# Copies for the weight sums, moves of key rows and the last stores issued by other engines than the loads

## The chip, the core and the metric

The kernel runs on one core of a Trainium2 chip. The metric is the device time of one execution in microseconds. A run's time is a little longer than the span in its profile, which goes from the first to the last instruction. A core has a matmul engine (TensorE, PE in the profile, with its weight loads as PEld), a vector engine (VectorE, DVE), an activation engine (ScalarE, ACT), a general engine (GpSimd, POOL) and SyncE (SP), which here only issues transfers. Each engine works through its own list of instructions in order. SyncE, ScalarE and GpSimd can each issue DMA transfers: the transfer itself is done by DMA engines, but the instruction that issues it stands in the issuing engine's list, and so does its wait.

## The reference, cut to what matters

Two layers over 528 tokens (16 learned ones and 512), each with two token mixers, a causal pooling and a latent attention with 8 heads:

```python
for l in range(DEPTH):                       # DEPTH = 2, D_MODEL = 1024
    h = rmsnorm(h_res, norm_gain[l])
    proj = h @ w_in[l]
    u_pool, z_pool, c_q, c_kv, k_rope, z_mla, g_pool, g_mla = jnp.split(proj, IN_SPLIT_POINTS, axis=-1)
    y_pool = (pool_mix(u_pool, pool_w_group[l], pool_scale[l]) * jax.nn.silu(z_pool)) @ pool_w_up[l]
    o_mla = mla(c_q, c_kv, k_rope, pos, g_qa, g_kva, w_q_b, w_kv_b, g_qn, g_kn)
    y_mla = (o_mla * jax.nn.silu(z_mla)) @ mla_w_up[l]
    merged = jax.nn.sigmoid(g_pool) * y_pool + jax.nn.sigmoid(g_mla) * y_mla
    h_res = h_res + merged @ w_out[l]
```

In `mla`, a head's key is 64 columns of its own and 32 rotated columns that all heads share; keys and queries are normalised per head.

## The kernel before, in words

Tokens lie along the free axis, features along the 128 partitions. Every product with a weight runs as three matmuls on halves of split numbers (`mm3`, L192, L195, L196): high by high, low by high, high by low.

**Weights.** A stream of products, `plan`, runs from the first projection to the last output. For each chunk of 128x512, `wload` has SyncE load 256 KB into one of three `raw` buffers (L115), ScalarE copies it to the high half `whi` (L187) and VectorE subtracts to get the low half `wlo` (L188). A load waits for a free `raw` buffer, which `wlo` gives back.

**The attention of a head.** `prep(h)` multiplies the head's key rows with a spread factor `bc` (L875), splits the product and moves the rotated query rows (L889). `head` computes scores, exponentials (L915, ScalarE) and has GpSimd scale the weights by their sums (`scale`, L922 and L923); `pv` transposes them on TensorE (L979) and multiplies with the values. Between these pieces the stream of products is run on (`gap`), so that TensorE always has work.

**Key rows.** `kn[p]` holds the own key columns of a pair of heads, 64 rows each; `kp` holds the rotated shared key in rows 64 to 128. For the even head of a pair, `lend` moves the first 64 rows of `kn[p]` into `kp` (L866) and the head reads `kp`. For the odd head, `prep` moves the shared rows from `kp` into the first 64 rows of `kn[p]` (L877) and the head reads `kn[p]`. There are 8 moves of each kind.

**Sums of weights.** Some products of the second layer's gates and of both output projections use sums and differences of weight blocks, so that fewer products are needed. `weight_sums` builds these sums in DRAM ahead of their use: 32 copies DRAM to DRAM (L356), and on top of each an adding transfer issued by GpSimd (L359). They are spread over the attention by `after(...)`.

**What sets the order.** Instructions are written in the order in which the Python code runs, with a clock of planned matmul time (`clk`). A list scheduler then sets the final order on each engine, and waits follow from the data. `behind(ins, other)` adds a wait for another instruction by hand, and `earlier(ns)` names the matmul that was written `ns` of planned time ago. So `behind(x, earlier(14000))` lets x go when TensorE has come to 14 us of planned time before the place where x was written.

**The end.** The last products, named "ob", store their results with `self.out(..., q)` (L1101) on a queue that `out_pairs` chooses; the earlier outputs go out on GpSimd.

Of the kernel before, what the change touches and what calls it, by code (L numbers as in the profile page):

```python
# [72 lines left out]
def trunk(ctx, tc, xT, pos, win, wkr, wqb, wkb, wvb, wgr, wpu, wmu, wout, gains, const, yT):  # L73
    nc = tc.nc
    pe, act, dve, gp, sp = nc.tensor, nc.scalar, nc.vector, nc.gpsimd, nc.sync
# [15 lines left out]
    def slot(tag, dt=F32, bufs=1, w=W):  # L91
        return sl.tile([P, w], dt, tag=tag, name=nm(tag), bufs=bufs)

    def tmp(w=W):
        return tp.tile([P, w], F32, tag="tmp", name=nm("tmp"), bufs=3)
# [95 lines left out]
    def mm3(out, wh, wl, xh, xl, start, stop, more=False, hold=False):  # L191
        first = pe.matmul(out, wh, xh, start=start, stop=False, skip_group_check=more)  # L192
        if hold:
            behind(first, newest[0])
        pe.matmul(out, wh, xl, start=False, stop=False, skip_group_check=more)  # L195
        newest[0] = pe.matmul(out, wl, xh, start=False, stop=stop, skip_group_check=more)  # L196
        past.append((clk[0], newest[0]))
# [3 lines left out]
    def earlier(ns):  # L201
        return next((m for c, m in reversed(past) if c <= clk[0] - ns), past[0][1])
# [99 lines left out]
    def split(hi, lo, src, a, b):  # L302
        act.activation(hi[:, a:b], src, AF.Copy)  # L303
        dve.tensor_sub(lo[:, a:b], src, hi[:, a:b].bitcast(F32))  # L304

    def behind(ins, other):
        tc.add_manual_dep(ins.ins, other.ins.name,
                          mybir.DependencyInfo(mybir.DependencyClass.Sync, mybir.DependencyReason.DATA))
# [38 lines left out]
    def weight_sums(name, w):  # L347
        def made(u, i):
            a, b = w[2 * u], w[2 * u + 1]
            d = wsum[name][u]  # L350
            src = {0: (b[:, 0:512], b[:, 512:1024]), 2: (a[:, 0:512], b[:, 0:512]), 1: (a[:, 0:512], d[:, 0, :]),
                   3: (a[:, 512:1024], d[:, 1, :])}
            return d[:, i, :], src[i]

        def copy(d, src):
            behind(sp.dma_start(d, src[0]), earlier(14000))  # L356

        def add(d, src):
            behind(gp.dma_start(d, src[1], accum_op=ALU.add), earlier(4000))  # L359

        for u in range(len(w) // 2):
            for fn, i in ((copy, 0), (copy, 2), (add, 0), (copy, 1), (add, 2), (add, 1), (copy, 3), (add, 3)):
                yield lambda fn=fn, u=u, i=i: fn(*made(u, i))

    class Layer:
# [497 lines left out]
            sp.dma_start(bc, kdr[self.l][h:h + 1, :].partition_broadcast(P))  # L863

        def lend(self, p):
            sp.dma_start(self.kp[0:64, :], self.kn[p][0:64, :])  # L866

        def prep(self, h):
            p, odd = h // 2, h % 2
            n0, r0 = (64, 0) if odd else (0, 64)  # L870
            kf = tmp()
            bc = self.bcs.pop(h)
            if h + 2 < H:
                self.spread_k(h + 2)
            dve.tensor_mul(kf, self.kn[p] if odd else self.kp, bc)  # L875
            if not odd:
                sp.dma_start(self.kn[p][0:64, :], self.kp[64:128, :])  # L877
            elif p < 3:
                self.lend(p + 1)
            kh, kl = slot("kh", F32R, bufs=2), slot("kl", F32R, bufs=2)  # L880
            split(kh, kl, kf[:, :T], 0, T)
            qh, ql = qhl[odd]
            x0 = self.x0
            src = self.qn[p][n0:n0 + 64, x0:T]
            act.activation(qh[n0:n0 + 64, x0:T], src, AF.Copy)
            dve.tensor_sub(ql[n0:n0 + 64, x0:T], src, qh[n0:n0 + 64, x0:T].bitcast(F32))
            g0 = 32 * (h % 4)
            for d, f in zip((qh, ql), self.qr[h // 4]):
                sp.dma_start(d[r0:r0 + 32, x0:T].bitcast(F32), f[g0:g0 + 32, x0:T].bitcast(F32))  # L889
            return kh, kl, qh, ql  # L890
# [252 lines left out]
        def out_pairs(self, nxt, name, products):  # L1143
            order = [(p, u) for p in products for u in range(2)]
            l = self.l
            a, b, c = self.halves()
            n = b - a
            A, B = (a, b), (b, c)
            src = []
            for p, u in order:  # L1150
                w0, w1 = wout[l, OUT[2 * u]], wout[l, OUT[2 * u + 1]]
                src.append({1: w0[:, 0:512], 2: w0[:, 512:1024], 4: w1[:, 512:1024]}.get(p))
                if src[-1] is None:
                    src[-1] = wsum[l][u][:, {5: 0, 6: 1, 7: 2, 3: 3}[p], :]
            bank = self.banks

            def grow(m, s, v):
                x = xb[:, m, s[0]:s[1]]
                dve.scalar_tensor_tensor(out=x, in0=v, scalar=0.5, in1=x, op0=ALU.mult, op1=ALU.add)

            def carry(m, s, v, u, scale, o):
                t = self.carried[u][:, o:o + n]
                act.activation(t, v, AF.Copy, scale=scale)
                gp.dma_start(xb[:, m, s[0]:s[1]], t, accum_op=ALU.add)

            def body(i, w):
                p, u = order[i]
                m0, m1 = OUT[2 * u:2 * u + 2]
                key = {2: "e", 7: "c", 4: "c"}.get(p, "a"), u
                if key not in bank:  # L1170
                    bank[key] = (sct if key[0] == "a" else mmt)()
                ps = bank[key][:, :n]
                t, o = (B if p == 3 else A), (0 if p == 1 else 4)
                for k in range(4):
                    xh, xl = (x[:, t[0]:t[1]] for x in self.mg[k + o]) if p < 4 else self.tt[k][p]
                    c_ = P * k
                    mm3(ps, w[0][:, c_:c_ + P], w[1][:, c_:c_ + P], xh, xl, k == 0 and p in (1, 2, 7), k == 3, True)
                    if k == 1:
                        yield 6 * (n / 2.4)
                q = sp if name == "ob" else gp  # L1180
                if p == 1:
                    self.carried[u] = slot("sv", bufs=2)
                    carry(m0, A, ps, u, 0.5, 0)
                elif p == 2:
                    grow(m0, A, ps)
                    self.out(m0, A, nxt, q)
                elif p == 7:
                    grow(m1, B, ps)
                elif p == 6:
                    carry(m1, A, ps, u, -0.5, HALF)  # L1190
                elif p == 5:
                    carry(m1, B, ps, u, -0.5, 0)
                    self.out(m1, B, nxt, q)
                    if u == 1 and not self.last:
                        for m in range(3):
                            nxt.square_x(m)
                elif p == 4:
                    grow(m1, A, ps)
                    self.out(m1, A, nxt, q)
                else:  # L1200
                    grow(m0, B, ps)
                    self.out(m0, B, nxt, q)
                    if not self.last:
                        nxt.square_x(m0)
                        nxt.square_x(m1)
                if i == len(order) - 1:
                    done.add((l, name))
                yield 6 * (n / 2.4)

            plan.append(Gemm((l, name), src, 512 * len(src), body=body))  # L1210
            plan[-1].more = True

# [236 lines left out]
```

## Time and profile before

| | us |
|---|---|
| median of 3 runs | 782.33 |
| lowest and highest of them | 780.72, 783.87 |
| the profiled execution | 782.78 |
| its span | 781.0 |

| engine | busy us | share of the span |
|---|---|---|
| TensorE | 774.8 | 99% |
| VectorE | 568.6 | 73% |
| ScalarE | 445.2 | 57% |
| GpSimd | 233.3 | 30% |

Busy time counts the records of instructions, issuing a DMA not included on SyncE and ScalarE. Matmul records overlap, so TensorE can lose a few tenths of a microsecond between two starts and still read as busy. A wait is named by who waited and for whom; SyncE has no work of its own, so its waits are those of its queue of transfers. The transfers that the change concerns, from the page's list of DMA issues (output <- input, issuing queue, count, size, median us from issue to landing):

```profile
wsum<-wout SPq DMA_DIRECT2D x16, 256.0 KB, 3.5
wsumgp<-win SPq DMA_DIRECT2D x16, 256.0 KB, 3.3
kp<-kn SPq DMA_DIRECT2D x8, 132.0 KB, 5.2
yT<-xb SPq DMA_DIRECT2D x4, 128.0 KB, 1.7
```

### The profile page before, as it was taken

How to read it: one execution, taken by the hardware profiler on the slowest of the kernel's cores; microseconds unless marked ns; L12 is line 12 of the kernel's file. 1: busy time of each engine (PE TensorE's matmuls, PEld its weight loads, DVE VectorE, ACT ScalarE, POOL GpSimd, SP SyncE). 2: the span in 40 equal slices, each digit the busy share in tenths (PEclk: the TensorE clock that was granted, in tenths of full speed). 3: DMA queues.
4: the chain of work that ended last, by engine and by line, in shares of the span. 5: the costliest groups of instructions: out<-in, count | busy, mean ns of one | idle time of the engine just before them, and what ended most of it. 6: DMA issues, size and time to landing. Idle time of an engine off the chain costs nothing.

```text
span 781.0 us, 15326 instructions
## 1 busy us (share of the span) xinstructions
PE 774.8 (99%) x5469; PEld 712.5 (91%) x5469; DVE 568.6 (73%) x1326; ACT 445.2 (57%) x1016; POOL 233.3 (30%) x303
## 2 busy tenths in 40 slices
PE   9999999999999999999999999999999999999998
PEld 9999899999999999999997898887788999988887
DVE  5848787446778876589764477865897888864984
ACT  7645555645566665645564356546667766664462
POOL 1024525103335333211330136221006625440213
PEclk9999999999999999999999999999999999999999
DMA  6242467765746465565662524425556666662655
GB/s 244 82 97 89 124 170 151 179 167 144 156 109 165 115 141 120 155 168 175 168 170 81 98 87 123 132 63 181 141 140 162 174 174 166 176 221 75 209 154 138
DMA packets 65325, 112.92 MB, mean 145 GB/s; under 512 B 10704, under 2 KB 15696, under 8 KB 65248
## 3 DMA queue, kind: packets, MB, share of 16 engines
q1 hardware_dynamic: 55344, 92.18, 40.0%
q0 software_dynamic: 8896, 17.92, 13.0%
q10 hardware_dynamic: 1008, 1.84, 0.6%
q8 instruction: 43, 0.70, 0.4%
q14 instruction: 34, 0.28, 0.1%
HBM read 100.18 MB, written 22.62 MB: 157 GB/s over the span
## 4 chain that ended last, share of the span: by engine, by line
PE 92%; DVE 3%; DMA 2%; ACT 1%; issue 1%; SPq 0%; DVEq 0%; ACTq 0%
PE mm L192 26%; PE mm L196 26%; PE mm L195 26%; PE S L192 3%; PE S L196 2%; PE S L195 2%; PE mm L979 2%; PE o L985 1%; PE o L984 1%; DVE wlo L188 1%; PE S L506 1%; DMA raw<-win 1%; PE mm L408 1%; DMA raw<-wsum 1%; PE mm L465 0%
## 5 line engine op out<-in xcount | busy, mean ns | idle before, releaser
L192 PE MATMUL mm<-hh,whi 128*128 128x264 f32 (+2 forms) x992 | 307.0, 312 | 0.1
L196 PE MATMUL mm<-hh,wlo 128*128 128x264 f32 (+2 forms) x992 | 304.7, 309 | 0.3 <-DVE wlo L188 0.2
L195 PE MATMUL mm<-hl,whi 128*128 128x264 f32 (+2 forms) x992 | 304.4, 308 | 0.0
L188 DVE TENSOR_TENSOR wlo<-raw,whi 128x512 fp32r<-128x512 f32 (+1 forms) x253 | 179.8, 714 | 103.7 <-ACT whi L187 101.2
L187 ACT ACTIVATE whi<-raw 128x512 fp32r<-128x512 f32 (+1 forms) x253 | 154.2, 612 | 166.4 <-PE mm L195 105.0
L192 PEld LDWEIGHTS mm<-hh,whi 128*128 128x128 f32 x992 | 186.6, 189 | 11.0 <-ACT racc L993 0.5
L195 PEld LDWEIGHTS mm<-hl,whi 128*128 128x128 f32 x992 | 187.2, 189 | 8.7
L196 PEld LDWEIGHTS mm<-hh,wlo 128*128 128x128 f32 x992 | 186.2, 188 | 9.4 <-DVE wlo L188 1.1
L922 POOL TENSOR_SCALAR pa<-pa,rs 128x272 f32<-128x272 f32 (+1 forms) x32 | 33.0, 1031 | 103.0 <-DVE rs L941 64.2
L922 POOL TENSOR_SCALAR cq<-cq,rs 128x400 f32<-128x400 f32 (+1 forms) x32 | 52.2, 1631 | 0.0
L192 PE MATMUL mm<-cq,whi 128*128 128x264 f32 (+2 forms) x140 | 43.8, 313 | 0.0
L195 PE MATMUL mm<-cq,whi 128*128 128x264 f32 (+2 forms) x140 | 43.7, 312 | 0.0
L196 PE MATMUL mm<-cq,wlo 128*128 128x264 f32 (+2 forms) x140 | 43.3, 312 | 0.1
L908 DVE CUSTOM_DVE_ANT_0 S<-S,maskw,nqs 128x272 f32<-128x272 f32 (+4 forms) x80 | 38.6, 497 | 5.2 <-PE S L196 4.9
L725 POOL TENSOR_TENSOR racc<-racc,tmp 128x264 f32<-128x264 f32 (+1 forms) x15 | 14.5, 964 | 84.9 <-ACT tmp L724 84.8
L304 DVE TENSOR_TENSOR tl<-mm,th 128x512 fp32r<-128x512 f32 (+1 forms) x64 | 30.0, 482 | 8.0 <-ACT th L303 6.3
L359 POOL DMA_DIRECT2D wsum<-wout x8 | 7.0, 873 | 91.7 <-PE mm L196 77.0
L303 ACT ACTIVATE th<-mm 128x512 fp32r<-128x512 f32 (+1 forms) x64 | 26.2, 432 | 10.2 <-PE mm L979 9.6
L915 ACT ACTIVATE cq<-S,bia 128x400 f32<-128x400 f32 (+2 forms) x48 | 24.4, 513 | 13.2 <-DVE bia L953 8.5
L192 PE MATMUL mm<-u,whi 128*128 128x264 f32 (+1 forms) x96 | 31.3, 326 | 0.0
L196 PE MATMUL mm<-u,wlo 128*128 128x264 f32 (+1 forms) x96 | 30.9, 322 | 0.0
L195 PE MATMUL mm<-kn,whi 128*128 128x264 f32 (+1 forms) x96 | 30.6, 320 | 0.0
(344 smaller groups left out, 1684.2 us busy)
## 6 DMA issues: line engine op xcount, KB each, us to landing
raw<-win SPq DMA_DIRECT2D x139, 256.0 KB, 2.9
raw<-wout SPq DMA_DIRECT2D x22, 256.0 KB, 3.5
bc<-kdr SPq DMA_DIRECT2D x16, 264.0 KB, 4.6
wsum<-wout SPq DMA_DIRECT2D x16, 256.0 KB, 3.5
raw<-wpu SPq DMA_DIRECT2D x16, 256.0 KB, 3.2
wsumgp<-win SPq DMA_DIRECT2D x16, 256.0 KB, 3.3
raw<-wmu SPq DMA_DIRECT2D x16, 256.0 KB, 2.8
raw<-wsumgp SPq DMA_DIRECT2D x16, 256.0 KB, 3.6
```

What stands on the lines that cost most here:

```text
L187: act.activation(hi[:, :n], raw[:, :n], AF.Copy)
L188: dve.tensor_sub(lo[:, :n], raw[:, :n], hi[:, :n].bitcast(F32))
L192: first = pe.matmul(out, wh, xh, start=start, stop=False, skip_group_check=more)
L195: pe.matmul(out, wh, xl, start=False, stop=False, skip_group_check=more)
L196: newest[0] = pe.matmul(out, wl, xh, start=False, stop=stop, skip_group_check=more)
L303: act.activation(hi[:, a:b], src, AF.Copy)
L304: dve.tensor_sub(lo[:, a:b], src, hi[:, a:b].bitcast(F32))
L725: self.acc_last = gp.tensor_add(self.acc[:, a:b], self.acc[:, a:b], t[:, :b - a])
L908: dve.tensor_tensor_reduce(out=sv, in0=sv, in1=mask, scale=nqs[:, i, h:h + 1], scalar=3e38, op0=ALU.add, op1=ALU.min, accum_out=bia[:, c:c ...
L915: act.activation(pv, sv, AF.Exp, scale=-1.0, bias=bia[:, i:i + 1], accum_out=rs[:, c:c + 1])
L922: gp.tensor_scalar(pt[i], pt[i], rs[:, i:i + 1], None, op0=ALU.mult)
L979: pe.transpose(tr[:, P * (i - j):P * (i - j + 1)], pt[i][:, NM + P * j:NM + P * (j + 1)], ident)
```

## The change

Four places change their issuing engine. The 32 copies for the weight sums go from SyncE to ScalarE, and the matmul that each waits for is 6 us back in planned time and no longer 14. The 16 moves of key rows go from SyncE to GpSimd, and each now also waits for the matmul 4 us back; before, they waited for their data alone. The 4 last stores go from SyncE to ScalarE. SyncE keeps the weight loads and the other small transfers. As the scheduler runs over the whole program again, the order of other instructions shifts in places too; the prediction shows three of them.

```diff
@@ weight_sums
         def copy(d, src):
-            behind(sp.dma_start(d, src[0]), earlier(14000))
+            behind(act.dma_start(d, src[0]), earlier(6000))
@@ Layer.lend
-            sp.dma_start(self.kp[0:64, :], self.kn[p][0:64, :])
+            behind(gp.dma_start(self.kp[0:64, :], self.kn[p][0:64, :]), earlier(4000))
@@ Layer.prep
             if not odd:
-                sp.dma_start(self.kn[p][0:64, :], self.kp[64:128, :])
+                behind(gp.dma_start(self.kn[p][0:64, :], self.kp[64:128, :]), earlier(4000))
@@ Layer.out_pairs, body
-                q = sp if name == "ob" else gp
+                q = act if name == "ob" else gp
```

## The prediction

> **What bounds the kernel now.** First the page, then three stretches of the span, to see whether TensorE ever waits.
>
> ```profile
> span 781.0 us, 15326 instructions
> PE 774.8 (99%) x5469; PEld 712.5 (91%) x5469; DVE 568.6 (73%) x1326; ACT 445.2 (57%) x1016; POOL 233.3 (30%) x303
> PE 92%; DVE 3%; DMA 2%; ACT 1%; issue 1%; SPq 0%; DVEq 0%; ACTq 0%
> ```
> ```profile
> 100.00:700.00 600.00, 599.42 (x4269) 554.41 (x4268) 446.39 (x1071) 350.21 (x821) 189.36 (x238) 1.00 0.57 147
> 700.00:781.00 81.00, 76.95 (x423) 65.65 (x422) 55.56 (x108) 34.98 (x71) 14.26 (x22) 1.00 0.48 143
> 600.00:700.00 100.00, 99.66 (x680) 91.34 (x679) 84.31 (x218) 69.05 (x181) 48.41 (x58) 1.00 0.69 185
> ```
> The columns behind the length are busy time of PE, PEld, DVE, ACT and POOL, then the granted clock. TensorE is busy in 599.42 of the 600 us in which every moved transfer but the last stores lies; it runs at full clock, and the chain that ended last is 92% TensorE and 0% of SyncE's queue. Busy time hides small gaps, because a matmul's record reaches over the start of the next, so I also look at starts below. The change touches no matmul. What it can give is a TensorE wait that a late load caused; what it can cost is a new one.
>
> Next the waits of SyncE's queue and of the engines (who waited <- for whom: us in total, times, longest).
>
> ```profile
> SPq L115 <- DVE wlo L188: 259.8, 140, 6.9
> SPq L356 <- PE mm L196: 36.6, 21, 5.7
> SPq L877 <- DMA kp<-kn: 23.7, 8, 4.0
> ```
> ```profile
> ACT whi L187 <- PE mm L195: 108.6, 94, 3.7
> DVE wlo L188 <- ACT whi L187: 106.6, 87, 5.8
> ACT whi L187 <- DMA raw<-win: 18.8, 13, 4.5
> ```
> The load queue stands 36.6 + 23.7 = 60.3 us behind the two steps that the change takes off it: copies that wait for a matmul (L356), and the move back of key rows that waits for the move before it (L877). But it waits 259.8 us for a free raw buffer, so much of the 60.3 us is time in which no load could go. ScalarE waited for a load of w_in only 18.8 us, and longer (108.6 us) for TensorE to free a split weight: weights are mostly ready early.
>
> **The change part by part. What it removes.** The order on SyncE late in layer 1 (bc is a head's spread key factor, kp and kn the key tiles, raw a weight buffer):
>
> ```order
>  L115 DMA raw_8548<-wsumgp_124 128x512
>  L863 DMA bc_8742<-kdr_122 128x528
> -L866 DMA kp_6464<-kn_1206_6712 64x528
>  L115 DMA raw_8568<-wsumgp_124 128x512
> -L877 DMA kn_1206_6712<-kp_6464 64x528
>  L115 DMA raw_8622<-win 128x512
>  L115 DMA raw_8644<-win 128x512
> ```
> Both moves leave; the two loads of w_in no longer stand behind the second. The trace has this place at 625 us: SyncE's timeline (start, length, what), a row of the chain, the landing times of L877 (us, min/median/max), and the usual landing of a load and of a move (DMA issues, last column).
>
> ```profile
> 625.58 0.50 SPq L866 DMA_DIRECT2D kp<-kn  x1
> 626.52 0.33 SPq L115 DMA_DIRECT2D raw<-wsumgp  x1
> 630.75 0.50 SPq L877 DMA_DIRECT2D kn<-kp  x1
> 631.35 1.57 SPq L115 DMA_DIRECT2D raw<-win  x2
> ```
> ```profile
> 631.35 5.68 DMA raw<-win
> ```
> ```profile
> DMA to landing us min/median/max: 2.2/2.9/5.9
> ```
> ```profile
> raw<-win SPq DMA_DIRECT2D x139, 256.0 KB, 2.9
> kn<-kp SPq DMA_DIRECT2D x8, 132.0 KB, 2.9
> ```
> The queue stands still from 626.85 to 630.75, and the load issued behind the move takes 5.68 us against a median of 2.9. TensorE pays a little later, at 638 and 644 us:
>
> ```profile
> 638.02 0.28 PE L195 MATMUL mm<-hl,whi 128*128 128x256 f32 x1
> 638.53 0.39 PE L196 MATMUL mm<-hh,wlo 128*128 128x256 f32 x1 [0.22 <-DVE wlo L188]
> 638.87 0.28 PE L195 MATMUL mm<-hl,whi 128*128 128x256 f32 x1
> 638.99 0.28 PE L196 MATMUL mm<-hh,wlo 128*128 128x256 f32 x1
> ```
> ```profile
> 644.35 0.49 PE L979 MATMUL mm<-cst,cq 128*128 128x128 f32 x3
> 644.91 0.50 PE L196 MATMUL mm<-hh,wlo 128*128 128x512 f32 x1
> ```
> At 638 the step takes 0.51 us where the same step takes 0.12 us: 0.39 us lost. At 644 the three transposes and the wait together take 0.56 us; I count 0.2 us of it (between 0 and 0.4) as lost. With the move gone the load lands about 5.68 - 2.9 = 2.8 us earlier, which covers both: **-0.6 us**. Once gone, the next thing late there is VectorE (84.31 of 100 us busy), so it can also stay. Elsewhere between 100 and 700 us TensorE is idle 600 - 599.42 = 0.58 us in all; for scattered late loads I take **-0.3 us** (0 to -0.6).
>
> The Trainium skill, page "DMA: Bandwidth & Descriptors", section "Issuing engines are not separate DMA queues", says that transfers from all issuers share the same 16 DMA engines and interleave, and that spreading them saves issue time only. By that rule the load at 631 us still shares its engines with the move, the 0.6 us stays, and the sum comes out 0.6 us higher; the trace has no load beside a move of another queue to decide it.
>
> **What it adds on ScalarE:** 32 copies (L356) and 4 stores. The issue is priced by L356 on SyncE (ns, min/median/max) and by the one kind of DMA that ScalarE issues today:
>
> ```profile
> L356 SPq DMA_DIRECT2D wsum<-wout x16: 496/519/1245, 92.8 to 648.7; - x16
> ```
> ```profile
> 601.29 0.62 ACT L885 ACTIVATE qhl<-q 64x512 fp32r<-64x512 f32 x1
> 601.48 0.33 ACTq L1069 DMA_DIRECT2D gate<-tc  x1
> 601.81 0.47 ACT L915 ACTIVATE pa<-S,bia 128x272 f32<-128x272 f32 x1
> ```
> The sequencer issues while the engine still executes the activation before it, and the next one starts on time. So 32 x 0.33 to 0.52 us = 10.6 to 16.6 us, most under ScalarE's own work, the rest in its idle 781 - 445.2 = 336 us: 0 on the path. Each copy now also waits on ScalarE for a matmul 6 us back in the planned order, not 14. Queued behind it are weight splits, evacuations and exponentials, for which VectorE and then TensorE wait. On SyncE such a wait is 36.6/21 = 1.7 us, but SyncE runs ahead of TensorE and ScalarE mostly behind it, so it is nearer to 0; that copies start later (8 us of planned time) is hidden by the sums' use in later stages.
>
> The re-planned order has one visible cost. On ScalarE, at the first use of the gated heads in layer 0 (q: split of the first 16 positions; whi_5000: a weight split):
>
> ```order
>  L187 ACTIVATE whi_4926<-raw_4924 128x512
>  L1061 ACTIVATE cq_872_4843<-cq_872_4843 128x264
> +L187 ACTIVATE whi_5000<-raw_4998 128x512
>  L303 ACTIVATE q_599_3358<-tmp_4871 128x16
>  L303 ACTIVATE q_702_3897<-tmp_4875 128x16
> -L187 ACTIVATE whi_5000<-raw_4998 128x512
> ```
> A weight split now stands ahead of the two short ones. The trace of ScalarE and TensorE there:
>
> ```profile
> 334.15 0.30 ACT L303 ACTIVATE q<-tmp 128x16 fp32r<-128x16 f32 x2
> 334.36 0.61 ACT L187 ACTIVATE whi<-raw 128x512 fp32r<-128x512 f32 x1
> ```
> ```profile
> 334.02 0.28 PE L196 MATMUL mm<-hh,wlo 128*128 128x264 f32 x1
> 334.40 0.51 PE L192 MATMUL mm<-q,whi 128*128 128x264 f32 x2
> ```
> TensorE's next matmul reads that q and already starts late by 0.26 us. With 0.61 us ahead of it: **+0.6 us** (0 to 0.9).
>
> **What it adds on GpSimd:** 16 moves. One late in layer 1 (pa, cq: attention weights being scaled, pm: their first columns):
>
> ```order
>  L922 TENSOR_SCALAR cq_1686_8793<-cq_1686_8793,rs_8796 128x400
>  L923 COPY pm_8526<-pa_8792 128x16
> +L877 DMA kn_1206_6712<-kp_6464 64x528
>  L923 COPY pm_8526<-cq_1686_8793 128x16
>  L922 TENSOR_SCALAR pa_8792<-pa_8792,rs_8796 128x144
> ```
> The move stands between scalings on which transposes (L979) depend; if its matmul isn't done, they wait with it. GpSimd's plain DMAs and the tightest pair of uses of kp and kn:
>
> ```profile
> L1105 POOL DMA_DIRECT2D scr<-xb x16 | 8.8, 549 | 23.5 <-DVE xb L1159 7.1 <-DVE xb L1092 6.0 <-DVE u L304 4.2
> ```
> ```profile
> xb<-sv POOLq DMA_DIRECT2D x6, 132.0 KB, 4.4
> ```
> ```profile
> 663.83 0.70 DVE L875 TENSOR_TENSOR tmp<-kp,bc 128x528 f32<-128x528 f32 x1
> 671.30 0.70 DVE L875 TENSOR_TENSOR tmp<-kn,bc 128x528 f32<-128x528 f32 x1
> ```
> 16 x 0.55 = 8.8 us of GpSimd's idle time. A move is now released around the head that uses kp and must land before the next head's product: 7.5 us at the tightest, and 0.55 to issue with 2.9 to 5.9 us to land fits. On the path 0 (bounds 0 and 8.8).
>
> **Last stores:**
>
> ```profile
> 774.21 4.11 SPq L1101 DMA_DIRECT2D yT<-xb  x4
> ```
> ```profile
> 770.45 0.36 ACT L1163 ACTIVATE sv<-S 128x256 f32<-128x256 f32 x1
> ```
> ScalarE has nothing after 770.8 us; the stores wait for VectorE's sums as before: 0.
>
> **Sum:** -0.6 - 0.3 + 0.6 = -0.3 us against the profiled 782.78 us (span 781.0 and 1.78 around it); from the median of the runs, 782.33, that is **782.0 us**. No change can be told by a measurement here that is under 0.5%, 3.9 us.
>
> **The rivals.** *Loads were the bound (faster).* If the chain's 2% DMA, 15.6 us, were waits of TensorE and a quarter to a third of it went, 776 to 778 us. For it: 60.3 us of a standing load queue. Against: TensorE idle 0.58 us in 600, and 0.39 us at the worst place.
>
> *ScalarE is held (slower).* Copies wait on ScalarE in the middle of heads, where it is 69.05% busy. Were each of the 32 held the 1.7 us of SyncE's waits, that is 54 us of ScalarE; a tenth of it on the path gives 787 to 788 us. It decides from 3.9/32 = 0.12 us a copy reaching TensorE. For it: VectorE waits 106.6 us for whi already. Against: the named matmul is usually past when ScalarE, which evacuates TensorE's results, comes to the copy.
>
> *Key rows come late (slower).* If each move held the scalings or the next head by its 0.55 us issue, 16 x 0.55 gives 791 us; it decides from 0.24 us a move. A mechanism of this kernel that would do it: descriptors written by GpSimd while VectorE, 84% busy, works. The Trainium skill, "SBUF — State Buffer", warns of this under "The 'DVE blocks DMA' trap" and reports 3.1 us where 0.62 us is usual. The trace speaks against much of it: GpSimd's 132 KB transfers land in 4.4 us beside the same VectorE, inside 7.5 us.
>
> *Nothing happens at all:* the load's 5.68 us come from other traffic and the re-planned split hides; 782.3 us.
>
> **How the numbers follow.** Forecast (782.0, within 0.5%) 0.73; nothing at all 0.06; loads bound 0.07; ScalarE held 0.09; key rows late 0.05. So faster 0.07, same 0.79, slower 0.14. The range, 778.6 to 786.2 us, is the 0.5% on either side of 782.33 with its 0.79: the ends of my unknown costs (-1.4 to +0.9) lie inside, and the ends of the two slower rivals are left out.
>
> **What would show it.** Right: SyncE's list of waits without L356 and L877; the load behind the old L877 near 3 us; gaps under 0.2 us near 638 and 644; a gap of 0.6 us or more before the first matmul that reads q near 334; TensorE idle still under 1 us from 100 to 700. Wrong: ACT L187 or L915 waiting behind L356 with TensorE idle after it; transposes L979 waiting for pa or cq behind a move; L875 waiting for a DMA.

## The result and the profile after

The changed kernel takes 787.67 us (median of 6 runs, 785.22 to 789.1), the kernel before 782.86 us (6 runs, 780.72 to 783.87). The ratio is 1.0062 (95% interval 1.0042 to 1.0083): slower by 4.8 us, and above the forecast range. The profiled execution took 789.1 us with a span of 787.3, 6.3 us longer than the span before.

The page of the changed kernel, the lines that were shown of before:

```profile
span 787.3 us, 15330 instructions
PE 774.8 (98%) x5469; PEld 712.3 (90%) x5469; DVE 571.4 (73%) x1326; ACT 446.2 (57%) x1016; POOL 238.0 (30%) x319
PE 82%; issue 8%; DVE 3%; DMA 3%; ACT 2%; POOL 1%; SPq 0%; ACTq 0%; POOLq 0%; DVEq 0%
```

TensorE has the same work to the tenth of a microsecond; it now stands idle 6 us longer. The load queue did lose its waits at L356 and L877: its first one is now

```profile
SPq L115 <- DVE wlo L188: 316.8, 155, 8.0
```

against 259.8 us before. So nearly all of the 60 us that were freed (57 us) turned into waiting for a raw buffer: the loads weren't held by what stood between them.

The stretches of the changed kernel (length; busy time of PE, PEld, DVE, ACT, POOL; clock, DMA share, GB/s):

```profile
100.00:700.00 600.00, 593.91 (x4231) 550.00 (x4230) 443.83 (x1057) 347.59 (x813) 192.73 (x252) 0.99 0.56 146
600.00:700.00 100.00, 98.56 (x678) 90.62 (x677) 84.28 (x221) 69.01 (x183) 50.63 (x66) 1.00 0.67 182
320.00:345.00 25.00, 20.88 (x151) 20.37 (x150) 11.86 (x34) 9.48 (x28) 1.66 (x2) 0.86 0.56 127
```

The last of them in the kernel before:

```profile
320.00:345.00 25.00, 24.90 (x201) 24.39 (x200) 16.77 (x44) 12.64 (x33) 3.63 (x5) 1.00 0.52 126
```

Between 100 and 700 us TensorE now idles 6.09 us, it was 0.58. Of that, 4.12 us lie between 320 and 345 us, where 151 matmuls start in place of 201: 50 starts at the usual 0.12 us are 6.0 us. So nearly all of the loss is one place. Setting the start of the n-th matmul of one trace against that of the n-th of the other gives the same: 6.1 us lost between 320 and 342 us, 2.6 us between 590 and 670 with 1.0 us regained in between, and 1.1 us gained at start-up, which varies by that much between executions.

The place is the first use of the gated heads, which the prediction spoke of. TensorE and ScalarE of the changed kernel (idle before and its releaser in brackets):

```profile
332.90 0.28 PE L196 MATMUL mm<-hh,wlo 128*128 128x264 f32 x1
337.30 0.81 PE L192 MATMUL mm<-q,whi 128*128 128x264 f32 x2 [4.12 <-ACT q L303]
```
```profile
333.75 1.15 ACT L187 ACTIVATE whi<-raw 128x512 fp32r<-128x512 f32 x2 [4.06 <-DMA raw<-wmu]
336.20 0.42 ACT L1061 ACTIVATE cq<-cq 128x264 f32<-128x264 f32 x1 [1.30 <-DVE cq L1060]
336.53 0.61 ACT L187 ACTIVATE whi<-raw 128x512 fp32r<-128x512 f32 x1
```

The names point at `q`, and the 0.61 us split ahead of it (336.53) is there as forecast. But ScalarE had already stood 4.06 us for a load of `mla_w_up` (wmu). Its row in the chain, of after and then of before:

```profile
327.90 5.77 DMA raw<-wmu
```
```profile
328.57 2.58 DMA raw<-wmu
```

Issued 0.67 us earlier, it lands 333.67 - 331.15 = 2.5 us later, and by the matmuls, which stand 1.1 us earlier here, 3.6 us. Then comes a second loss. The windows of the changed kernel:

```profile
334.00:338.00 4.00, 0.70 (x3) 0.70 (x4) 3.56 (x10) 2.48 (x7) 0.00 (x0) 0.65 0.50 148
338.00:342.00 4.00, 4.00 (x20) 4.00 (x20) 1.85 (x9) 0.95 (x3) 0.00 (x0) 0.50 0.25 66
```

After the gap the granted clock is 0.50, and 20 matmuls start in 4 us where 35 did. From 337.30 to 342.0 us a step takes 0.22 us instead of 0.12: (0.10 / 0.22) x 4.7 = 2.1 us lost. The gap is 4.40 us from start to start (332.90 to 337.30), 4.28 us more than a usual step. Gap and clock make 4.28 + 2.1 = 6.4 us, against 0.26 us lost here before.

What is near that load: the kernel's DMA issues by L356 between 322 and 334 us, with their landing times below; before, the last copy went at 315.8 us and no L356 is in that window.

```profile
L356 ACTq DMA_DIRECT2D wsumgp<-win x2: 498/545/592, 324.1 to 325.5; - x2
DMA to landing us min/median/max: 4.0/4.3/4.7
```

And the share of the DMA engines in use, of before and then of after:

```profile
326.00:330.00 4.00, 4.00 (x35) 4.00 (x34) 3.37 (x10) 3.40 (x12) 0.51 (x1) 1.00 0.27 82
330.00:334.00 4.00, 4.00 (x34) 3.95 (x33) 2.77 (x8) 1.71 (x4) 1.13 (x2) 1.00 0.92 186
```
```profile
326.00:330.00 4.00, 4.00 (x35) 4.00 (x34) 2.66 (x8) 3.11 (x10) 1.59 (x2) 1.00 0.78 209
330.00:334.00 4.00, 3.18 (x26) 2.93 (x24) 0.42 (x1) 0.25 (x1) 0.07 (x1) 1.00 0.99 219
```

In the kernel before, GpSimd's adds at 329.5 and 330.4 us already filled the DMA engines to 0.92 behind the loads. Two copies that start 8 us of planned time later fill much of what was free ahead of that: loads, copies and adds now run together. Part of the step from 0.27 to 0.78 is the 1.1 us by which the changed kernel stands earlier; the kernel before at the same place of the program, 1.1 us later, is at 0.48:

```profile
327.00:331.00 4.00, 4.00 (x36) 4.00 (x35) 3.02 (x9) 2.87 (x8) 1.47 (x2) 1.00 0.48 165
```

### The profile page after: what moved, and what is told of

It is laid out like the page before. It is cut to its first block, busy times and chain, and to the rows that moved or that the text cites. A ratio compares the mean times of both kernels' runs of the same rounds, so it can differ in the third digit from the quotient of the medians.

```text
span 787.3 us, 15330 instructions
## 1 busy us (share of the span) xinstructions
PE 774.8 (98%) x5469; PEld 712.3 (90%) x5469; DVE 571.4 (73%) x1326; ACT 446.2 (57%) x1016; POOL 238.0 (30%) x319
## 4 chain that ended last, share of the span: by engine, by line
PE 82%; issue 8%; DVE 3%; DMA 3%; ACT 2%; POOL 1%; SPq 0%; ACTq 0%; POOLq 0%; DVEq 0%
PE mm L192 23%; PE mm L196 23%; PE mm L195 23%; PE S L192 2%; PE S L195 2%; PE S L196 2%; PE mm L979 2%; DVE wlo L188 1%; PE o L985 1%; PE o L984 1%; ACT whi L187 1%; DMA raw<-wmu 1%; PE S L506 1%; DMA raw<-wsumgp 1%; PE mm L408 1%
## 5 line engine op out<-in xcount | busy, mean ns | idle before, releaser
L192 PE MATMUL mm<-hh,whi 128*128 128x264 f32 (+2 forms) x992 | 306.5, 311 | 1.5 <-ACT whi L187 0.9
L192 PEld LDWEIGHTS mm<-hh,whi 128*128 128x128 f32 x992 | 186.3, 188 | 12.8 <-ACT whi L187 1.3
L922 POOL TENSOR_SCALAR pa<-pa,rs 128x272 f32<-128x272 f32 (+1 forms) x32 | 30.0, 936 | 97.0 <-DVE rs L941 62.6
L192 PE MATMUL mm<-cq,whi 128*128 128x264 f32 (+2 forms) x140 | 43.8, 313 | 0.0
L192 PE MATMUL mm<-q,whi 128*128 128x264 f32 (+1 forms) x96 | 31.0, 336 | 4.1 <-ACT q L303 4.1
L192 PE MATMUL mm<-u,whi 128*128 128x264 f32 (+1 forms) x96 | 31.2, 326 | 0.0
L196 PE MATMUL mm<-q,wlo 128*128 128x264 f32 (+1 forms) x96 | 31.1, 329 | 0.0
```

The costliest lines, as they stand in the source:

```text
L922: gp.tensor_scalar(pt[i], pt[i], rs[:, i:i + 1], None, op0=ALU.mult)
```

## The experiments

Three theories. **A**: the shorter distance puts the last copies beside the loads at 328 us, and the transfers share the DMA engines. **B**: ScalarE as issuer costs, wherever the copies stand. **C**: GpSimd's moves cause the collision. Each kernel was compared with the kernel before on the same chip.

| kernel | median us | before | ratio, interval | wmu load us | starts 320 to 345 |
|---|---|---|---|---|---|
| before | | | 1 | 2.58 | 201 |
| the change | 787.67 | 782.86 | 1.0062, 1.0042 to 1.0083 | 5.77 | 151 |
| e1 all, copies 14 us back | 782.69 | 781.69 | 1.0011, 1.0002 to 1.0020 | 2.53 | 202 |
| e2 copies only | 784.66 | 781.69 | 1.0039, 1.0025 to 1.0052 | 5.33 | 159 |
| e3 moves only | 783.53 | 781.69 | 1.0024, 1.0015 to 1.0032 | 2.70 | 199 |
| e4 copies on SyncE, 6 back | 783.14 | 781.69 | 1.0019, 1.0010 to 1.0027 | 4.12 | 188 |
| f1 last four copies 14 back | 783.93 | 781.62 | 1.0025, 1.0015 to 1.0035 | 2.77 | 199 |
| f3 last two copies issued earlier | 784.25 | 781.62 | 1.0031, 1.0020 to 1.0042 | 2.50 | 202 |
| f4 two adds left out | 787.17 | 781.62 | 1.0069, 1.0054 to 1.0084 | 3.73 | 173 |
| e6 copies on ScalarE 14 back, moves on SyncE | 781.61 | 781.62 | 1.0000, 0.9991 to 1.0009 | 2.57 | 201 |
| g1 as e1, moves without the wait | 781.05 | 781.82 | 0.9990, 0.9981 to 0.9999 | 2.52 | 201 |
| g2 as g1, moves on ScalarE | 782.67 | 781.82 | 1.0014, 1.0005 to 1.0023 | 2.54 | 201 |
| g3 as g1, wait at L866 | 781.41 | 782.14 | 0.9993, 0.9984 to 1.0002 | 2.49 | 202 |
| g4 as g1, wait at L877 | 782.14 | 782.14 | 1.0000, 0.9992 to 1.0009 | 2.74 | 199 |

**e1: the changed kernel with the old distance.**

```diff
-            behind(act.dma_start(d, src[0]), earlier(6000))
+            behind(act.dma_start(d, src[0]), earlier(14000))
```

> The changed kernel, but each copy for the sums waits on ScalarE for the matmul 14 us back in planned time, as it did on SyncE, and not 6. Theory A (the shorter distance put the last copies and the adding transfers behind them next to the loads of mla_w_up at 328 us; those land in 6 us, TensorE stands 4.3 us and then runs at half clock): the last copies are issued before 318 us, the loads at 328 us land in about 2.6 us, the gap before the first matmul on q is under 0.5 us, no half clock, and the time is 781 to 783.5 us. Theory B (ScalarE as issuer, or moves on GpSimd, are the cost, wherever the copies stand): 786 to 789 us.

The stall is gone, and the time lies in A's range. **e2: of the change, the copies' line alone.**

> The kernel before with the copies alone moved to ScalarE, 6 us back; moves and last stores stay on SyncE. Theory A: the same stall near 333 us and half clock after it, 786 to 789 us. Theory C (the moves on GpSimd delay the adding transfers and so cause the collision): no stall, 781 to 784 us.

The stall is there without any move on GpSimd: 3.58 us of idle and half clock behind it in the trace. The median, 3.0 us above before, misses the 786 us of theory A, because the stall isn't equally long in every execution. Five of the 12 runs had a mean granted clock of 1.000 and took 782.49 to 783.60 us; seven had 0.996 to 0.998 and took 784.37 to 787.83 us. All six runs of the change had 0.996 to 0.998. **e3: of the change, the moves alone.**

> The kernel before with the moves of key rows alone put on GpSimd. Theory A: no stall near 333 us beyond the 0.3 us of before, and the two small gaps near 638 and 644 us go; 781.5 to 783.5 us. Theory C: the stall near 333 us is there, 786 us or more.

No stall at 334, but 1.84 us from elsewhere (783.53 us, at the upper end of A's range). In the medians 3.0 + 1.8 is the whole 4.8 us of the change; as e2's median lies between two groups of runs, the fit is not to be read to the tenth. **e4: the kernel before with its copies still on SyncE and only the distance shortened.**

```diff
-            behind(sp.dma_start(d, src[0]), earlier(14000))
+            behind(sp.dma_start(d, src[0]), earlier(6000))
```

> The kernel before with only the distance of the copies changed, from 14 us to 6 us, still on SyncE. Theory A: the copies come late here too, now in the loads' own queue and ahead of the loads of mla_w_up, so a stall near 333 us of 2 us or more, 785 to 792 us. Theory B (ScalarE as issuer is the cost): 781 to 784 us.

The chain of e1, of e2 and of e4 at the load:

```profile
329.04 2.53 DMA raw<-wmu
```
```profile
327.84 5.33 DMA raw<-wmu
```
```profile
327.69 4.12 DMA raw<-wmu
```

A's mechanism holds: the distance alone delays the load even from the loads' own queue. Its numbers don't: TensorE's gap is under the 2 us expected, and 783.14 us lies in the range of theory B. In e4 the weight split stands behind `q`, as in the kernel before. TensorE's gap there:

```profile
335.06 0.51 PE L192 MATMUL mm<-q,whi 128*128 128x264 f32 x2 [1.64 <-ACT q L303]
```

C falls, by e2. B falls as the main cause, by e1. But the queue may have a part: with copies issued at nearly the same times (324.3 and 325.7 us in e4, 324.1 and 325.5 in e2), the load takes 4.12 us where they share its queue and 5.33 us where they have one of their own, one trace each. The first of the copies also lands sooner in the loads' queue (3.4 us in e2; neither trace gives a landing for the second). e4's row of L356 there has

```profile
DMA to landing us min/median/max: 2.9/2.9/2.9
```

**f1 and f3: is it these copies, and not the late copies in general?** In f1 the last four copies of layer 0 wait 14 us back and the other 28 wait 6; in f3 the last two are issued together with the two before them, at the distance of 6.

> The changed kernel, but the last four copies of layer 0's stream (the sums of w_in for position 3) wait for a matmul 14 us back instead of 6; the other 28 copies stay at 6, the moves stay on GpSimd. Theory A (only the copies that stand next to the loads of mla_w_up near 328 us cost, because their transfers and the adds share the DMA engines with these loads): loads there land in under 3.5 us, no TensorE gap over 1 us near 333, full clock after it, 782 to 783.5 us. Rival B (late copies cost everywhere, a little each): the gap goes or stays, but the time stays at 785 us or more.

> The changed kernel, but the last two copies for position 3 of layer 0's sums are issued together with the two before them, some 5 us of planned time earlier each; the wait stays 6 us back. Theory A: it is the collision of the very last copies with the loads at 328 us; without them the loads land in 2.5 to 4 us, the gap near 333 is under 1.5 us, 782 to 784 us. Rival B (wait distance itself): no change from 786 to 788 us.

Both take the stall away (load and starts in the table), and the split ahead of `q` with it. The times, 783.93 and 784.25 us, are just above A's ranges and below B's 785 and 786 us. What is left, 2.3 and 2.6 us, is near the 1.84 us of e3, so the other late copies cost nothing that shows beside e3. Against e1 it is 1.3 and 1.6 us more; f1's interval overlaps e1's and f3's only touches it, so a small cost of theirs isn't excluded.

**f4: copies or adds?** Of the four adds of the last position, those with odd number are left out. One of them stood at 329.0 us, so one add is left beside the loads.

> The changed kernel without the last two adding transfers of layer 0's stream (two sums of w_in then lack their second part); copies stay at 324 and 325.5 us and the split that was put ahead of q stays there. If the copies alone slow the loads of mla_w_up (A1): loads at 328 us still take 5 us or more, gap of 3 us or more near 333. If it needs the adds as well (A2): loads take 3 to 4 us, gap under 2 us, no stretch at half clock, about 783 to 784 us; what is left of the gap is then the 0.6 us of the split and the rest of the slower load.

The load takes 3.73 us, as A2 expected. So with two adds and no late copies it takes 2.5 to 2.8 us (before, e1, f1), with the copies and one add 3.73, with the copies and both adds 5.33 to 5.77: the second add costs this load some 2 us, but only beside the copies. There is no run with the copies and no add. The windows of f4:

```profile
334.00:338.00 4.00, 2.78 (x17) 2.78 (x18) 3.77 (x15) 2.53 (x8) 0.00 (x0) 0.82 0.50 149
338.00:342.00 4.00, 4.00 (x28) 4.00 (x27) 0.77 (x2) 0.00 (x0) 0.00 (x0) 0.76 0.13 48
```

The expected "no stretch at half clock" was wrong, after an idle of only 2.00 us:

```profile
335.22 0.51 PE L192 MATMUL mm<-q,whi 128*128 128x264 f32 x2 [2.00 <-ACT q L303]
```

The time was missed too. By the starts f4 loses 3.4 us near 334, 2.7 less than the change, but its median (of only four runs, 785.25 to 788.75 us) is no better; its trace has a wait of 1.33 us for `pa` near 596 us, where the changed kernel waits 0.36. Why isn't settled, so f4 counts for the landing and the clock only.

**e6: copies and last stores on ScalarE at the old distance, moves left on SyncE.**

> The kernel before with the copies on ScalarE at the old distance of 14 us and the last stores on ScalarE; the moves of key rows stay on SyncE. Theory A with the moves as a second small cost (1 to 2 us): equal to before, 781 to 782 us, ratio 0.998 to 1.001. Rival B (ScalarE as issuer costs, 32 x 0.12 us or more): 784 us or more. Rival C (the copies on SyncE held loads): faster than before by over 1 us.

The time of before, within 0.7 us either way. ScalarE as issuer costs nothing that shows, and the loads gain nothing from a queue without copies: rivals B and C of the expectation both fall.

**g1 to g4: why do the moves cost?** All four have the copies of e1.

```diff
-            behind(gp.dma_start(self.kp[0:64, :], self.kn[p][0:64, :]), earlier(4000))
+            gp.dma_start(self.kp[0:64, :], self.kn[p][0:64, :])
-                behind(gp.dma_start(self.kn[p][0:64, :], self.kp[64:128, :]), earlier(4000))
+                gp.dma_start(self.kn[p][0:64, :], self.kp[64:128, :])
```

That is g1; g2 has `act` in place of `gp`; g3 and g4 keep one of the two waits.

> Copies on ScalarE 14 us back (harmless so far), moves of key rows on GpSimd but without the added wait for the matmul 4 us back, so they wait for their data alone. Theory P (the issue itself costs: 0.6 to 0.8 us of GpSimd in front of scalings that TensorE's transposes wait for): still 782.5 to 783.5 us, with a gap of about 0.5 us at a transpose that reads pa near 592. Rival W (the added wait holds GpSimd): 781.3 to 782.0 us and no such gap.

> As the one before, but the moves are issued by ScalarE, again waiting for their data alone: SyncE keeps loads and small transfers only, and GpSimd gets nothing new. Theory P: no gap at a transpose that reads pa behind a move; 781 to 782 us, equal to before, or up to 1 us faster if late loads near 638 and 644 go (step a of the prediction). Rival W': the moves cost by their place among ScalarE's work (a move back waits for the move before it, 3 to 4 us at worst, with weight splits queued behind): 783 us or more, with waits of whi or th behind a move.

Theory P falls, by g1: GpSimd issues all 16 moves and the kernel is as fast as before, even a little faster (0.77 us; the interval ends at 0.9999; 781.05 us is just under rival W's range). Against e1, whose interval doesn't touch g1's, the added wait costs about 1.6 us. What the wait does is seen in the row of L877, of e3 and then of g1 (issue in ns, first and last start):

```profile
L877 POOL DMA_DIRECT2D kn<-kp x8: 547/596/783, 168.7 to 659.5; - x8
```
```profile
L877 POOL DMA_DIRECT2D kn<-kp x8: 530/554/984, 85.5 to 631.5; - x8
```

Before, they went from 85.2 to 630.8. With the wait each move goes into the list much later, and comes to stand ahead of scalings. GpSimd and the TensorE wait behind it in the changed kernel:

```profile
593.59 0.78 POOL L877 DMA_DIRECT2D kn<-kp  x1
594.19 1.20 POOL L922 TENSOR_SCALAR pa<-pa,rs 128x272 f32<-128x272 f32 x1
```
```profile
597.63 0.44 PE L979 MATMUL mm<-cst,pa 128*128 128x128 f32 x2 [0.36 <-POOL pa L922]
```

This row isn't proof: g1 has a gap at that transpose too in its profile (1.18 us, against rival W's "no such gap"), with no move ahead of it but with longer scalings, and e2, with no move on GpSimd at all, waits 0.39 us there. The times are the proof.

The larger loss is elsewhere. Start against start, TensorE loses 2.3 us in e3, 1.5 in e1 and 1.6 in the changed kernel between 620 and 637 us, but 0.03 us in g1 and 0.1 in e6. It waits there for weight splits and for `tmp`, behind a load of `w_in` issued near 610 us that takes 7.91 us in e3 and 7.10 in e1 (before 6.1, g1 3.6). The load's row in e3's chain, then ScalarE's and TensorE's waits there:

```profile
610.19 7.91 DMA raw<-win
```
```profile
618.19 0.63 ACT L187 ACTIVATE whi<-raw 128x512 fp32r<-128x512 f32 x1 [2.06 <-DMA raw<-win]
```
```profile
624.99 0.50 PE L192 MATMUL mm<-hh,whi 128*128 128x512 f32 x1 [0.63 <-DVE tmp L644]
```

So here too a load that lands late is in the chain; whether it is the cause, and what in the new order slows it, wasn't tested. g2 leaves SyncE and GpSimd free of moves and is 1.6 us slower than g1. That is the mechanism of rival W', though 782.67 us is under the 783 us it gave: the move back waits on ScalarE for the move before it, and ScalarE's own work with it.

```profile
246.82 0.49 ACTq L877 DMA_DIRECT2D kn<-kp  x1
247.36 0.31 ACT L972 ACTIVATE pmr<-pm 128x128 fp32r<-128x128 f32 x1 [3.93 <-DMA kp<-kn]
```

> Copies on ScalarE 14 us back, moves on GpSimd; only the move into kp (L866) also waits for the matmul 4 us back, the move back (L877) for its data alone. Theory L (the later move into kp near 608 us pushes the loads of 610 to 613 us, and with them the splits that TensorE waits for at 617 to 625 us): 782.5 us or more, gaps at 620 to 625 us. Theory K (the move back is the one that costs: its wait puts it 8 to 80 us later, among scalings and loads): 781 to 781.6 us and no such gaps.

> The reverse: only the move back (L877) waits for the matmul 4 us back, the move into kp for its data alone. Theory K: 782.5 us or more, a gap of about 0.5 us at a transpose that reads pa near 592. Theory L: 781 to 781.6 us.

g3's trace has no wait at the transpose, and 0.22 us at the later L192 where g4 and e3 wait 0.51 and 0.63. The rows of g3, and of g4:

```profile
623.49 0.50 PE L192 MATMUL mm<-hh,whi 128*128 128x512 f32 x1 [0.22 <-DVE tmp L644]
```
```profile
592.28 0.44 PE L979 MATMUL mm<-cst,pa 128*128 128x128 f32 x2 [0.37 <-POOL pa L922]
624.12 0.50 PE L192 MATMUL mm<-hh,whi 128*128 128x512 f32 x1 [0.51 <-DVE tmp L644]
```

These rows lean to the move back (theory K), but between 620 and 637 us g3 and g4 lose nearly the same, 0.7 and 0.8 us. And the ratios, 0.9993 and 1.0000, have intervals that overlap each other and g1's, and neither reaches the 782.5 us that was expected of the guilty one; how the 1.6 us divide stays open.

## Why the prediction was wrong

**The step that failed** is the half sentence on ScalarE's copies: that they start later "is hidden by the sums' use in later stages". That is true of the sums, and they weren't late. It looked at who reads the copies, not at who shares the DMA engines with them. Instead of 0, the later start cost some 6 us in the trace of the change, and 3.0 us in the medians of e2: the load of `mla_w_up` took 5.77 us and not 2.58, and the clock halved behind the gap. f1 shows that it belongs to the last four copies. A row that could have told it was in the profile before: 0.92 of the DMA engines in use at 330 to 334 us.

**Put at ScalarE's door.** The prediction looked for the cost of the copies in ScalarE's list. The issue (10.6 to 16.6 us, hidden) was rightly put at 0: e6's interval, 0.9 thousandths either side, allows 0.02 us for each of 32 copies. The rival "ScalarE is held" had the right time, 787 to 788 us, by luck, as its mechanism was another: ScalarE stood for the DMA, not behind L356. Its condition, 0.12 us a copy on the path, wasn't met.

**The split ahead of q, +0.6 (0 to 0.9).** The place was right and the 0.61 us are there, but TensorE loses 4.28 us at the gap, because a late load stands in front, and the clock behind it wasn't in the sum. The split goes with the stall: in the traces of the change, e2 and f4, the three with half clock, it is ahead of `q`; in e1, e4, f1 and f3 it is behind, as before. It may decide on the clock: f4's load takes 0.4 us less than e4's, but its gap is 0.4 us longer (2.00 against 1.64 us). No run changes the split alone, so its share isn't shown.

**The rule of the Trainium skill** in "DMA: Bandwidth & Descriptors", section "Issuing engines are not separate DMA queues", was weighed at the wrong place, the moves at 631 us (0.6 us). The runs agree with it at 328 us: transfers from ScalarE and GpSimd slow a load from SyncE from 2.6 to 5.8 us, and e6 gains nothing from the separate queue. The 1.2 us between e4 and e2, whose edits differ in the copies' queue alone, isn't covered by it.

**Late loads near 638 and 644, -0.6.** They went: matmuls regain about 1.0 us between 638 and 653 in e3 and after. That they went because the moves left SyncE isn't shown: e6 keeps the moves there and already regains 0.6 us, so at most 0.4 us is theirs. The further -0.3 us isn't seen.

**Moves on GpSimd, 0.** Wrong by 1.8 us (e3), inside its bounds of 0 to 8.8. The price was sought in the issue, which g1 shows to be free; it was the added wait, which the text counted as harmless. "Key rows come late" named the scalings, and the transposes did wait for `pa`, but for 0.4 us only, and its mechanism, a slow issue, falls.

**Last stores, 0:** right, by e6, which has them on ScalarE. **Loads were the bound:** fell as argued; 60 us less standing of the load queue gave nothing. **The 0.5%** under which no change was to be told was too wide: the intervals here reach 0.1 to 0.2% either way.

## What to carry to other kernels

Before moving a background transfer in time, look at the DMA share of the stretch where it will land, and at which load is in flight there with little slack; its own reader being far away says nothing. A hand-made wait does more than hold an instruction: a scheduler moves the instruction to where the wait is met, so price the new place. Freeing a queue brought nothing here, where its first wait was for a free buffer.

## What the runs showed of the hardware

In these traces TensorE's clock halves around short idling. The granted clock was half for 6.8 us with an idle stretch of 4.12 us (the change), and for 3.4 us with one of 3.58 us (e2) and of 2.00 us (f4). In the changed kernel it fell 2 us into the gap, in e2 and f4 only 1.1 and 1.3 us after TensorE had started again. With a gap of 1.64 us (e4) it stayed whole:

```profile
334.00:338.00 4.00, 2.94 (x24) 2.94 (x25) 3.88 (x15) 2.43 (x8) 0.00 (x0) 1.00 0.52 152
338.00:342.00 4.00, 4.00 (x35) 4.00 (x35) 1.80 (x5) 1.11 (x2) 0.00 (x0) 1.00 0.27 70
```

In the change and f4 that is 2.1 and some 1.5 us on top of the wait. That it doesn't come in every execution is seen in e2: five runs with a mean clock of 1.000 beside seven below it. The Trainium skill, "TensorE: Matmul & The Clock Gate", Part 1, gives free-running windows of about 3.4 us and a fall to half rate after one idle window. The lengths agree (6.8 is two of them); that 2.00 us sufficed in f4 shows that TensorE need not be idle for as long as a window.

A transfer's queue may matter as well as its neighbours: the same copies at nearly the same time cost a load 1.2 us less from the load's own queue (4.12 against 5.33 us), one execution each, so this is a hint and not shown.
